# New places for four packed matmul operands, and sixty products that nothing reads

## The chip, the cores and the metric

The kernel runs on one core of one Trainium2 chip. The metric is the device time of one execution in microseconds: the median of the runs of one kernel. One more execution is taken by the hardware profiler; it gives the profile, with times in microseconds from the span's start. TensorE is PE in the profile (PEld is its weight load), VectorE is DVE, ScalarE is ACT, GpSimd is POOL, and SP issues most DMAs.

## What is computed

One layer of a hybrid decoder on 256 tokens, with 16 learned meta tokens in front (272 in all) and 2048 channels, all in float32. The mixer runs two branches on one normalised input: forgetting attention (FoX, 8 heads) and gated linear attention (GLA, 4 heads). Then comes a squared-ReLU MLP of width 8192.

```python
def hybrid_mixer(xn, w_in, b_forget, w_alpha2, b_alpha, gla_norm_g, w_o_fox, w_o_gla, w_out):
    proj = xn @ w_in
    ...
    o_fox = forgetting_attention(fq, fk, fv, ff, b_forget)
    g_log = jax.nn.log_sigmoid((ga @ w_alpha2 + b_alpha).astype(jnp.float32)) / GLA_TAU
    o_gla = gated_linear_attention(gq, gk, gv, g_log)
    o_gla = (head_rmsnorm(o_gla, gla_norm_g) * jax.nn.silu(gr.astype(jnp.float32))).astype(xn.dtype)
    y = jax.nn.sigmoid(gate_fox) * (o_fox @ w_o_fox) + jax.nn.sigmoid(gate_gla) * (o_gla @ w_o_gla)
    return y @ w_out

# reference: h = h + hybrid_mixer(rmsnorm(h), ...);  h = h + squared_relu_mlp(rmsnorm(h), w1, w2)
# squared_relu_mlp: jnp.square(jax.nn.relu(xn @ w1)) @ w2;  at the end rmsnorm(h)[:, N_META:]
```

## The kernel before

**Layout.** Activations stand transposed: channels on the 128 partitions, tokens along the free dimension. A matrix of 2048 rows is 16 row tiles (KT = 16), and the weights come from the host as a stream of 128-column chunks in the order of use; `chunk` counts them. `next_weights` takes the next chunk in two halves of 8 row tiles: SP loads a half (512 KB) into `raw`, ScalarE rounds it to `hi` (L124), and VectorE forms the remainder `lo = raw - hi` (L125), both as float32r. Five `raw` and five `wt` buffers let this run ahead of TensorE.

**Products.** Every activation is split in the same way into a high and a low part that stand side by side, so that one product can stream both. `gemm2` runs 16 steps, and each step (`mac2`) is a pair: `hi` of the weights against high and low activation together, 512 columns (L140), and `lo` against the high activation, 256 columns (L141).

```python
    def mac2(ps, hi, lo, x, first, last):
        nc.tensor.matmul(ps, hi, x, start=first, stop=False)
        nc.tensor.matmul(ps[:, 0:NT], lo, x[:, 0, :], start=False, stop=last)
```

`gemm_all` works on all 272 tokens with three products a step (L157 to L159). The result lies in one accumulator bank of 512 columns, from the pool `pg` (3 banks, the big products) or `px` (5 banks, the small ones). `total` or `add_residual` adds its two halves (ScalarE copies one, VectorE adds).

**The four packed operands.** Besides `x`, the first normalised input, four activations serve as the streamed operand of `gemm2`: `og` (the gated attention's output), `y` (the mixer's sum), `x2` (the second normalised input) and `a` (the squared-ReLU output, made anew for each of four groups of the MLP). Each is 16 pieces of 512 floats, high part and low part without a gap. Two storage slots hold them, one after the other: `s1` holds `x`, then `y`, then `a`; `s2` holds first some scratch, then `og`, then `x2`. In the built program `s1` begins 64 bytes past a multiple of 256 and `s2` 160 bytes past one. `operand` cuts a slot into pieces by a table of places, and `steps` makes that table: piece k starts at `first + 512 * k` floats plus one of four numbers, one for each quarter of the pieces. Before, those four are 0, 64, 128 and 192 floats, all whole multiples of 256 bytes, so that all 16 pieces of a use have one place modulo 256 bytes.

`og` is read by 16 products of 16 pairs (256 pairs), `y` by 16 (256), `x2` by 64 (1024), each of the first three `a` by 16 (256) and the last `a` by 12 (192); its last four output columns go another way, with L850 and L859.

**Order.** The stages run one after the other: the first chunks with the loading of the input, four GLA heads, eight FoX heads, the two output projections with their gates, the product with `w_out`, and four groups of the MLP, each of 16 up and 16 down products. Small work is put off with `later(n, fn)` and issued after n further products; `flush()` issues what is left. `gla_head` ends with `scale`, where `spread` (L223) turns the norm factors (`diag`, VectorE, L220) into a bank from which ScalarE copies `rg` (L586); VectorE then scales `oT` (L589, L591) and both engines split it into `og` (L173, L174). After the fourth head come `flush()`, `og_tile()` and the FoX heads. Within each engine a scheduler of the compiler orders the instructions, so that neighbours in the code can stand apart.

Of the kernel before, what the change touches and what calls it, by code (L numbers as in the profile page):

```python
# [16 lines left out]
P = 128  # L17
# [48 lines left out]
def trunk(ctx: ExitStack, tc: tile.TileContext, hT, w_small, w_all, consts, w_alpha2, out):  # L66
    nc = tc.nc
    serial = [0]

    def nm(s):  # L70
        serial[0] += 1
        return f"{s}_{serial[0]}"
# [7 lines left out]
    px = ctx.enter_context(tc.tile_pool(name="px", bufs=5, space=PSUM))  # L80
# [3 lines left out]
    def bank(pool, s):  # L84
        return pool.tile([P, 512], F32, tag="bank", name=nm(s))
# [7 lines left out]
    def issued():  # L93
        for e in list(waiting):
            e[0] -= 1
            if e[0] <= 0:
                waiting.remove(e)
                e[1]()

    def flush():  # L100
        while waiting:
            issued()
# [26 lines left out]
    def next_weights(keep_hi=None):  # L129
        c = chunk[0]  # L130
        chunk[0] += 1
        parts = []
        for i in range(2):
            hi, lo, step = weight_half(c, i, None if keep_hi is None else keep_hi[:, HK * i : HK * (i + 1), :])
            step(0, HK)
            parts.append((hi, lo))
        return lambda k: (parts[k // HK][0][:, k % HK, :], parts[k // HK][1][:, k % HK, :])
# [5 lines left out]
    def gemm2(w, x, k0=0, nk=KT):  # L143

        ps = bank(pg, "ps")
        for k in range(nk):
            hi, lo = w(k0 + k)
            mac2(ps, hi, lo, x[k], k == 0, k == nk - 1)
        issued()
        return ps  # L150

    def gemm_all(w, x, n=NA):

        ps = bank(pg, "psa")
        for k in range(KT):
            hi, lo = w(k)
            nc.tensor.matmul(ps[:, 0:n], hi, x[:, k, 0, :], start=(k == 0), stop=False)  # L157
            nc.tensor.matmul(ps[:, 0:n], lo, x[:, k, 0, :], start=False, stop=False)  # L158
            nc.tensor.matmul(ps[:, 0:n], hi, x[:, k, 1, :], start=False, stop=(k == KT - 1))  # L159
        issued()  # L160
        return ps

    def total(ps, t=None):

        b = tmp.tile([P, NT], F32, tag="evb", name=nm("evb"))
        nc.scalar.copy(b, ps[:, NT:512])  # L166
        if t is None:
            t = tmp.tile([P, NT], F32, tag="evt", name=nm("evt"), bufs=4)
        nc.vector.tensor_tensor(t, ps[:, 0:NT], b, op=ALU.add)  # L169
        return t  # L170
# [54 lines left out]
    def operand(pool, name, size, places, tag):  # L225


        t = pool.tile([P, size], F32R, tag=tag, name=nm(name))
        rows = []
        for at, gap in places:  # L230
            both = t[:, at : at + 2 * gap].rearrange("p (o t) -> p o t", t=gap) if at + 2 * gap <= size else None
            rows.append(both[:, :, 0:NT])
        return rows

    S1, S2 = 8728, 8628
    def steps(first, *by):
        return [(first + 512 * k + by[k * len(by) // KT], NT) for k in range(KT)]

    AT_OG = steps(8, 0, 64, 128, 192)
    AT_Y = steps(48, 0, 64, 128, 192)  # L240
    AT_X2 = steps(40, 0, 64, 128, 192)
    AT_A = [steps(e, 0, 64, 128, 192) for e in (16, 40, 12, 58)]


    h = keep.tile([P, KT, NA + 3], F32, name="h")
    x = keep.tile([P, KT, 2, NA], F32R, tag="s1", name="x")
# [79 lines left out]
    for s in range(KT // 2):  # L326
# [3 lines left out]
        for kk in range(2):  # L330
            k = 2 * s + kk
# [10 lines left out]
            for c, (hi, lo) in enumerate(at):  # L342
                ps = first_ps[c]
# [5 lines left out]
            for c, (hi, lo) in enumerate(at):  # L349
                ps = first_ps[c]  # L350
# [83 lines left out]
    def og_tile():  # L434
        if not og_box:
            og_box.append(operand(keep, "og", S2, AT_OG, "s2"))
        return og_box[0]

    def gla_gates(ts):
        sg = att.tile([P, 4, NT], F32, tag="sg", name=nm("sg"))  # L440
        for i in range(4):
            t = ts[i] if ts else total(gemm2(next_weights(), xt))
            nc.vector.tensor_tensor(t, t, rbt, op=ALU.mult)
            nc.scalar.activation(sg[:, i, :], t, AF.Sigmoid)
            nc.vector.tensor_tensor(sg[:, i, :], sg[:, i, :], t, op=ALU.mult)
        return sg
# [13 lines left out]
    def gla_head(hd, sg, ready=None):  # L460
# [135 lines left out]
        if sg is None:  # L596
            sg = gla_gates(None)
            st["sg"] = sg
            scale()
        else:  # L600
            st["sg"] = sg
            later(4, scale)
# [8 lines left out]
    ps = gemm_all(lambda k: (small[k // HK][0][:, k % HK, :], small[k // HK][1][:, k % HK, :]), x)  # L611
    norm1_spread()
    nc.vector.tensor_tensor(ga[0:16, :], ps[0:16, 0:NA], rb[0:16, :], op=ALU.mult)
    nc.vector.tensor_tensor(fl, ps[32:40, 0:NA], rb[32:40, :], op=ALU.mult)
    sg0 = gla_gates(ts[0:4])
    table = nc.scalar.preload_act_table_set("natural_log_exp_and_others")
    tc.keep_in_program_order(table)
# [9 lines left out]
    for hd in range(1, GLA_H):  # L627
        gla_head(hd, None)
    flush()
    og = og_tile()  # L630


# [112 lines left out]
    for j0 in range(0, KT, 2):  # L745
        gates = ahead if j0 == 0 else [gate() for _ in range(4)]
        w = next_weights()
        for j in range(2):
            t = total(gemm2(w, oft, k0=8 * j, nk=8))
            nc.vector.tensor_tensor(gates[2 * j], gates[2 * j], t, op=ALU.mult)  # L750
        for j in range(2):
            t = total(gemm2(next_weights(), og))
            nc.vector.tensor_tensor(t, gates[2 * j + 1], t, op=ALU.mult)
            nc.vector.tensor_tensor(yf[:, j0 + j, :], gates[2 * j], t, op=ALU.add)
    y = operand(keep, "y", S1, AT_Y, "s1")
    for j in range(KT):
# [5 lines left out]
    ht = h[:, :, NM:NA]  # L762
    x2 = operand(keep, "x2", S2, AT_X2, "s2")

# [58 lines left out]
    for g in range(NG):  # L823
        a = operand(keep, "a", S1, AT_A[g], "s1")
        held = []
        for f in range(KT):
            ps = gemm2(next_weights(), x2)
# [18 lines left out]
    for n in range(NL):  # L846
        j, ps = KT - NL + n, bank(pg if n < 3 else px, "ps")
# [42 lines left out]
    v, p, none = nc.vector, nc.gpsimd, lambda: None  # L890
# [72 lines left out]
```

## Time and profile before

| | |
|---|---|
| time, median of 2 runs | 1631.84 us (1631.83 to 1631.86) |
| profiled execution | 1631.39 us, span 1629.7 us |
| granted TensorE clock, mean | 0.996 |
| busy: TensorE, weight load | 1612.4 us, 1450.3 us |
| busy: VectorE, ScalarE, GpSimd | 1048.0, 793.7, 91.2 us |
| read from memory | 289.19 MB, 179 GB/s over the span |

Busy time of TensorE is not its pace: matmuls are pipelined, and their ends are modelled. The pace is the time from one start to the next. In the view of windows a row has the stretch, its length, and then for each engine the busy time and the number of instructions (x) that touch the stretch, the granted clock, the busy share of the DMA engines and GB/s.

### The profile page before, as it was taken

Reading aid. Unit: us, or ns where it says so; the run is one execution under the profiler, and the core shown is the slowest. Engines: PE = TensorE matmul, PEld = TensorE weight load, DVE = VectorE, ACT = ScalarE, POOL = GpSimd, SP = SyncE. Lnnn points to the kernel's source line nnn. Section 1 sums busy time; section 2 is a strip of 40 time slices with the busy share of each in tenths; the row PEclk is TensorE's granted clock in tenths of the full one; section 3 lists DMA queues with packets and bytes.
Section 4 is the critical chain, followed back from the end, with each engine's and each line's share of the span. In section 5 each row is a group of like instructions: output and inputs, shape, how many; then the busy total and the mean of one; then the engine's idle time right before and its main releaser. Section 6 shows DMA issues by size and latency. Waiting matters only on the chain.

```text
span 1629.7 us, 25555 instructions
## 1 busy us (share of the span) xinstructions
PE 1612.4 (99%) x9996; PEld 1450.3 (89%) x9996; DVE 1048.0 (64%) x1591; ACT 793.7 (49%) x1217; POOL 91.2 (6%) x144
## 2 busy tenths in 40 slices
PE   8999999999999999999999999999999999999997
PEld 7999999999998888888888888888888888888886
DVE  6766757476556566665677776567656776667655
ACT  6555444454445444444565444444444444444563
POOL 0100000010000000000011000000000000000012
PEclk9999999999999999999999999999999999999998
DMA  8444555454455555555555555555555555555552
GB/s 290 156 143 156 165 161 165 157 195 157 157 161 173 184 191 190 187 191 189 188 189 189 183 190 182 190 186 190 178 197 193 184 188 188 191 184 190 185 193 66
DMA packets 90265, 292.97 MB, mean 180 GB/s; under 512 B 9096, under 2 KB 21648, under 8 KB 89888
## 3 DMA queue, kind: packets, MB, share of 16 engines
q1 hardware_dynamic: 87552, 288.88, 54.1%
q8 instruction: 79, 1.29, 0.3%
q10 hardware_dynamic: 2416, 1.33, 0.3%
q0 software_dynamic: 176, 1.12, 0.2%
q14 instruction: 42, 0.34, 0.1%
HBM read 289.19 MB, written 2.11 MB: 179 GB/s over the span
## 4 chain that ended last, share of the span: by engine, by line
PE 98%; DMA 1%; DVE 0%; ACT 0%; issue 0%; SPq 0%; DVEq 0%; ACTq 0%
PE ps L140 50%; PE ps L141 26%; PE psa L159 5%; PE psa L158 5%; PE psa L157 5%; PE ps L345 1%; PE ps L859 1%; DMA h<-hT_dram 1%; PE pa L506 1%; PE ps L850 0%; PE ps L352 0%; PE po L570 0%; DMA raw<-w_all_dram 0%; PE pz L404 0%; ACT x L332 0%; PE po L571 0%
## 5 line engine op out<-in xcount | busy, mean ns | idle before, releaser
L125 DVE TENSOR_TENSOR wt<-raw,wt 128x1024 fp32r<-128x1024 f32 x522 | 644.7, 1235 | 330.0 <-ACT wt L124 320.0
L124 ACT CAST wt<-raw 128x1024 fp32r<-128x1024 f32 x522 | 548.7, 1052 | 397.3 <-issue 158.6
L140 PE MATMUL ps<-x,wt 128*128 128x512 f32 x1952 | 688.4, 395 | 0.0
L141 PE MATMUL ps<-x,wt 128*128 128x256 f32 x1952 | 551.3, 282 | 0.0
L140 PEld LDWEIGHTS ps<-x,wt 128*128 128x128 f32 x1952 | 366.8, 188 | 83.1
L141 PEld LDWEIGHTS ps<-x,wt 128*128 128x128 f32 x1952 | 367.9, 188 | 0.0
L140 PE MATMUL ps<-a,wt 128*128 128x512 f32 x960 | 336.8, 394 | 0.0
L141 PE MATMUL ps<-a,wt 128*128 128x256 f32 x960 | 270.8, 282 | 0.0
L140 PEld LDWEIGHTS ps<-a,wt 128*128 128x128 f32 x960 | 180.7, 188 | 41.0
L157 PE MATMUL psa<-x,wt 128*128 128x272 f32 x640 | 187.3, 293 | 0.0
L159 PE MATMUL psa<-x,wt 128*128 128x272 f32 x640 | 184.8, 289 | 0.0
L158 PE MATMUL psa<-x,wt 128*128 128x272 f32 x640 | 184.4, 288 | 0.0
L141 PEld LDWEIGHTS ps<-a,wt 128*128 128x128 f32 x960 | 181.5, 189 | 0.0
L166 ACT COPY evb<-ps 128x256 f32<-128x256 f32 x160 | 59.3, 373 | 237.6 <-PE ps L141 235.4
L169 DVE TENSOR_TENSOR evt<-ps,evb 128x256 f32<-128x256 f32 x158 | 66.9, 424 | 107.1 <-ACT evb L166 106.9
L157 PEld LDWEIGHTS psa<-x,wt 128*128 128x128 f32 x640 | 120.3, 188 | 0.7
L158 PEld LDWEIGHTS psa<-x,wt 128*128 128x128 f32 x640 | 120.4, 188 | 0.2
L159 PEld LDWEIGHTS psa<-x,wt 128*128 128x128 f32 x640 | 120.4, 188 | 0.1
L140 PE MATMUL ps<-y,wt 128*128 128x512 f32 x256 | 89.4, 393 | 0.0
L140 PE MATMUL ps<-og,wt 128*128 128x512 f32 x256 | 89.1, 394 | 0.0
L775 ACT COPY evb<-ps 128x256 f32<-128x256 f32 x76 | 28.3, 372 | 113.0 <-PE ps L141 112.9
L141 PE MATMUL ps<-y,wt 128*128 128x256 f32 x256 | 71.7, 280 | 0.0
(261 smaller groups left out, 1396.1 us busy)
## 6 DMA issues: line engine op xcount, KB each, us to landing
raw<-w_all_dram SPq DMA_DIRECT2D x537, 512.0 KB, 3.9
raw<-w_all_dram SPq DMA_DIRECT2D x7, 384.0 KB, 6.8
h<-hT_dram SPq DMA_DIRECT2D x1, 1100.0 KB, 10.0
negc<-fdram POOLq DMA_DIRECT2D x1, 1088.0 KB, 6.0
out_dram<-h SPq DMA_DIRECT2D x3, 256.0 KB, 2.6
out_dram<-h ACTq DMA_DIRECT2D x3, 256.0 KB, 3.1
h<-hT_dram SPq DMA_DIRECT2D x1, 550.0 KB, 7.3
raw<-w_all_dram SPq DMA_DIRECT2D x2, 256.0 KB, 4.4
```

Source lines behind the costliest of these rows:

```text
L124: nc.scalar.copy(hi[:, k, :], r)
L125: nc.vector.tensor_tensor(lo[:, k, :], r, hi[:, k, :].bitcast(F32), op=ALU.subtract)
L140: nc.tensor.matmul(ps, hi, x, start=first, stop=False)
L141: nc.tensor.matmul(ps[:, 0:NT], lo, x[:, 0, :], start=False, stop=last)
L157: nc.tensor.matmul(ps[:, 0:n], hi, x[:, k, 0, :], start=(k == 0), stop=False)
L158: nc.tensor.matmul(ps[:, 0:n], lo, x[:, k, 0, :], start=False, stop=False)
L159: nc.tensor.matmul(ps[:, 0:n], hi, x[:, k, 1, :], start=False, stop=(k == KT - 1))
L166: nc.scalar.copy(b, ps[:, NT:512])
L169: nc.vector.tensor_tensor(t, ps[:, 0:NT], b, op=ALU.add)
L345: nc.tensor.matmul(ps, hi, x[:, k, :, NM:NA], start=st, stop=False)
L506: nc.tensor.matmul(dst, k[:, a, :], q[:, a, :], start=(a == 0), stop=(a == 1))
L775: nc.scalar.copy(b, ps[:, NT:512])
```

## The change

All tables of places change, and a function `pace` is added that runs once, after `flush()`.

```diff
-    AT_OG = steps(8, 0, 64, 128, 192)
-    AT_Y = steps(48, 0, 64, 128, 192)
-    AT_X2 = steps(40, 0, 64, 128, 192)
-    AT_A = [steps(e, 0, 64, 128, 192) for e in (16, 40, 12, 58)]
+    AT_OG = steps(0, 8, 22, 42, 58)
+    AT_Y = steps(0, 6, 22, 36, 52)
+    AT_X2 = steps(0, 10, 26, 44, 60)
+    AT_A = [
+        steps(0, 8, 24, 38, 54),
+        steps(0, 10, 26, 40, 56),
+        steps(0, 12, 28, 42, 60),
+        steps(0, 14, 30, 44, 62),
+    ]
...
+    def pace():
+        flat = x.rearrange("p k o t -> p (k o t)")
+        ps, other = bank(px, "pace"), bank(px, "pace")
+
+        def run(w0, m0, m=P, n=512, step=1, rows=P, banks=(ps,), mv=None):
+            if mv is None:
+                mv = flat[0:rows, m0 : m0 + n * step : step]
+            for i in range(4):
+                nc.tensor.matmul(banks[i % len(banks)][0:m, 0:n], flat[0:rows, w0 : w0 + m], mv, start=True, stop=True)
+
+        run(32, 4128)
+        run(48, 4128)
+        run(48, 4144)
+        run(32, 4144)
+        run(32, 4128, m=32)
+        run(32, 4112, m=32)
+        run(32, 4112)
+        run(32, 4128, n=256)
+        run(32, 4128, n=256, m=32)
+        run(32, 4128, n=128)
+        run(32, 4128, n=128, m=32)
+        run(32, 4128, rows=64)
+        run(32, 4128, step=2)
+        run(32, 4128, banks=(ps, other))
+        run(32, 0, mv=flat[:, 4128:4130].unsqueeze(1).to_broadcast([P, 256, 2]))
...
     flush()
+    pace()
     og = og_tile()
```

With the slots' starts, the places in bytes modulo 256 of the four quarters are:

| operand | before | after |
|---|---|---|
| `og` | 192 | 192, 248, 72, 136 |
| `y` | 0 | 88, 152, 208, 16 |
| `x2` | 64 | 200, 8, 80, 144 |
| `a`, first to fourth group | 128; 224; 112; 40 | 96, 160, 216, 24; 104, 168, 224, 32; 112, 176, 232, 48; 120, 184, 240, 56 |

Each form of `pace` is four products with weights and streamed columns both from `x`, into a bank that nothing reads. The forms differ in the places of the two operands, the number of weight columns (128 or 32), of streamed columns (512, 256, 128), of rows (128 or 64), in the step between columns, in the banks, and in the last one two columns are repeated 256 times by a zero step.

On TensorE, at the end of the last GLA head, the order before goes from the head's last product (`ps`) to the first FoX product (`psa`), and L223 for that head (`pr`) stands 36 products further on, inside it:

```order
L140 MATMUL ps_3453<-x,wt_3449 128x512
L141 MATMUL ps_3453<-x,wt_3449 128x256
L157 MATMUL psa_3545<-x,wt_3536 128x272
L158 MATMUL psa_3545<-x,wt_3536 128x272
L159 MATMUL psa_3545<-x,wt_3536 128x272
...
L223 MATMUL pr_3417<-diag_3493,ones 128x256
```

After the change the same place reads as follows (L452 is the product in `pace`; behind a tile's name stand the weight columns and the streamed columns):

```order
L141 MATMUL ps_3453<-x,wt_3449 128x256
L452 MATMUL pace_3514<-x 128x512 x16
L452 MATMUL pace_3514<-x 32x512 x8
L452 MATMUL pace_3514<-x 128x512 x4
L223 MATMUL pr_3417<-diag_3493,ones 128x256
L452 MATMUL pace_3514<-x 128x256 x4
L452 MATMUL pace_3514<-x 32x256 x4
L452 MATMUL pace_3514<-x 128x128 x4
L452 MATMUL pace_3514<-x 32x128 x4
L452 MATMUL pace_3514<-x 128x512 x9
...
L157 MATMUL psa_3607<-x,wt_3598 128x272
```

The sixty stand between the two products as one block, and L223 has moved out of the first FoX product into the block, behind its 28th. On ScalarE, behind the copy of that last GLA product (`evb`), the row of work before was:

```order
L166 COPY evb_3486<-ps_3453 128x256
L124 CAST wt_3662<-raw_3661 128x8x128
L444 ACTIVATE sg_3234<-evt_3488 128x256
L124 CAST wt_3667<-raw_3666 128x8x128
L586 COPY rg_3233<-pr_3417 128x256
L124 CAST wt_3740<-raw_3739 128x8x128
L173 CAST og_1299<-oT_3231 128x256 x4
```

and it now is (later lines lie 31 lower, so that L475 and L617 are L444 and L586 of before):

```order
L166 COPY evb_3486<-ps_3453 128x256
L124 CAST wt_3724<-raw_3723 128x8x128
L475 ACTIVATE sg_3234<-evt_3488 128x256
L617 COPY rg_3233<-pr_3417 128x256
L173 CAST og_1299<-oT_3231 128x256 x4
L124 CAST wt_3729<-raw_3728 128x8x128
L124 CAST wt_3802<-raw_3801 128x8x128
```

Ahead of the casts into `og` there are now one half of weights (L124) instead of three; the other two stand behind them.

## The prediction, made before the result

> **What bounds the kernel now.** I read the page first: busy shares, granted clock, the chain that ended last.
>
> ```profile
> PE 1612.4 (99%) x9996; PEld 1450.3 (89%) x9996; DVE 1048.0 (64%) x1591; ACT 793.7 (49%) x1217; POOL 91.2 (6%) x144
> PEclk9999999999999999999999999999999999999998
> PE 98%; DMA 1%; DVE 0%; ACT 0%; issue 0%; SPq 0%; DVEq 0%; ACTq 0%
> PE ps L140 50%; PE ps L141 26%; PE psa L159 5%; PE psa L158 5%; PE psa L157 5%; PE ps L345 1%; PE ps L859 1%; DMA h<-hT_dram 1%; PE pa L506 1%; PE ps L850 0%; PE ps L352 0%; PE po L570 0%; DMA raw<-w_all_dram 0%; PE pz L404 0%; ACT x L332 0
> ```
>
> TensorE works 1612 of 1629.7 us at full granted clock, and its own matmuls are 98% of the chain. The second view is TensorE's waits, all of them:
>
> ```profile
> PE pn L223 <- DVE diag L220: 3.5, 1, 3.5
> PE ps L345 <- ACT wt L293: 3.0, 1, 3.0
> PE pn L878 <- ACT sq L866: 1.5, 1, 1.5
> PE warm L318 <- DVE ones L192: 1.3, 1, 1.3
> PE ps L345 <- DVE x L333: 1.0, 1, 1.0
> ```
>
> They come to 10.3 us, and their lines are the start (L318, L345) and the norm at the very end (L878, and the one L223 whose output is `pn`). Between them TensorE waits for nobody. So what is put into the middle of TensorE's program lengthens the kernel one for one, and a matmul form that streams faster or slower moves the end by just as much. The time is the number of products times the pace of each.
>
> A duration in the page is not that pace: the 512-wide product "lasts" 395 ns, but the next starts long before. So I take start to start. The third view is the timeline in one `og` product, its first and its last step of sixteen:
>
> ```profile
> 521.56 0.39 PE L140 MATMUL ps<-og,wt 128*128 128x512 f32 x1
> 521.79 0.27 PE L141 MATMUL ps<-og,wt 128*128 128x256 f32 x1
> 521.91 0.40 PE L140 MATMUL ps<-og,wt 128*128 128x512 f32 x1
> ...
> 526.76 0.40 PE L140 MATMUL ps<-og,wt 128*128 128x512 f32 x1
> ```
>
> One step is a pair, 512 columns against the high weights (L140) and 256 against the low ones (L141). Fifteen pairs lie between 521.56 and 526.76: **346.7 ns a pair**, some 230 ns of it for the 512 (521.56 to 521.79) and 117 for the 256.
>
> **Part 1: the places.** Do places matter at all? The fourth view counts instructions on one operand in stretches where it alone is multiplied: `y` (810:890), `x2` (1260:1340), then the four uses of `a`.
>
> ```profile
> 810.00:890.00 80.00, 80.00 (x460) 70.06 (x459) 0.42 (x1) 0.33 (x1) 1.00 0.57 191
> 1260.00:1340.00 80.00, 80.00 (x458) 70.12 (x457) 0.00 (x0) 0.00 (x0) 1.00 0.57 187
> 990.00:1070.00 80.00, 80.00 (x455) 69.48 (x454) 0.42 (x1) 0.40 (x1) 1.00 0.57 187
> 1170.00:1250.00 80.00, 80.00 (x463) 70.92 (x462) 0.42 (x1) 0.40 (x1) 1.00 0.59 191
> 1350.00:1430.00 80.00, 80.00 (x459) 69.92 (x458) 0.42 (x1) 0.00 (x0) 1.00 0.57 188
> 1526.00:1590.00 64.00, 64.00 (x364) 56.70 (x363) 0.42 (x1) 0.40 (x1) 1.00 0.58 190
> ```
>
> About two of each TensorE count straddle the window's ends; half the rest are pairs. With the place in bytes modulo 256 (slot start plus the table's number):
>
> - `og`, place 192: 346.7 ns; 256 pairs
> - `y`, place 0: 80/229 = 349.3; 256 pairs
> - `x2`, place 64: 80/228 = 350.9; 1024 pairs
> - `a`, place 128: 80/226.5 = 353.2; place 224: 80/230.5 = 347.1; place 112: 80/228.5 = 350.1; 256 pairs each
> - `a`, place 40: 64/181 = 353.6; 192 pairs
>
> The same instruction at the same clock, with nothing waiting, differs by 2% from operand to operand, and the plainest thing that differs is the place. Weighted, these 2496 pairs take 874.3 us, 350.3 ns each.
>
> The change scatters them over 28 places, all multiples of 8; 192, 224 and 112 are among them, the other 25 are new. What a new place costs no row shows. From both sides by the nearest rows: all at the best pace seen (346.7) gives 865.4 us, **9 us less**; all at the worst (353.6) gives 882.6, **8 us more**. I see no order in the seven numbers that I would trust (112 and 128 are neighbours and differ by 3 ns), so I take for each new place their plain mean, 350.1, the middle of the two ends. Then `og` loses 0.9 us (256 x 3.4 ns), the second `a` 0.8, `y` 0.2; `x2` gains 0.8 (1024 x 0.8 ns), the uses at 128 and 40 gain 0.8 and 0.7, and `a` at 112 stays: the sum is **-0.4 us, between -9 and +8**. Behind them 192 single products of the tail (L850, L859) read the last `a` too; 3 ns each way would be 0.6 us, and I leave it in the range. Twenty-five independent draws also average out: the seven paces scatter by 2.7 ns, `x2` has its 1024 pairs in four draws of 256 and the rest have 64 or 48 in each, which makes 1.6 us of scatter in the sum.
>
> One rule speaks against any effect. The Trainium skill, "TensorE: Matmul & The Clock Gate", section "Step-by-step: what each phase is for", gives TensorE two independent read ports, so that loading the next weights takes nothing from the running matmul; an operand's place would then be indifferent. The rows above do not bear that out: 346.7 against 353.6 ns. By the rule the term is 0 instead of -0.4, so the sum would be 0.4 us higher.
>
> The writers of these tiles (L173, L174, L795, L796) also write to other places. In the trace ScalarE and VectorE are at 49% and 64%, no L140 or L141 stands among TensorE's waits, and these writes do not set the end; I cost them at nothing. If the cover went, it would show as a wait on these lines.
>
> **Part 2: the sixty products.** Each form is four products. They read `x`, complete since the first stage, and write two accumulator banks that are free. By the order they stand where TensorE went straight from L141 to L157, so there is no gap for them to fill:
>
> ```profile
> 333.04 0.39 PE L140 MATMUL ps<-x,wt 128*128 128x512 f32 x1
> 333.27 0.28 PE L141 MATMUL ps<-x,wt 128*128 128x256 f32 x1
> 333.39 0.29 PE L157 MATMUL psa<-x,wt 128*128 128x272 f32 x1
> ```
>
> All of their time counts. Eleven forms are 512 wide (44 products), two 256 (8), two 128 (8).
>
> - 512 wide: the rows above give 230 or 231 ns (333.04 to 333.27): 44 x 0.231 = **10.2 us**.
> - 256 wide: 333.27 to 333.39 is 120 ns and in `og` 117; 8 x 0.119 = **1.0 us**.
> - 128 wide: only the plain fp32 transposes are as narrow:
>
> ```profile
> 358.12 0.27 PE L696 MATMUL pv<-cons,vT 128*128 128x128 f32 x1
> 358.23 0.27 PE L697 MATMUL pv<-cons,vT 128*128 128x128 f32 x1
> 358.34 0.27 PE L698 MATMUL pv<-cons,vT 128*16 128x128 f32 x1
> ```
>
> 110 ns each. I take 110 for the four with 128 weight columns and 70, between that row and half a 256, for the four with 32: **0.7 us**.
>
> Sum **11.9 us**. What no row shows: 32 weight columns, 64 rows, a stride of two, a pair of columns repeated by a zero step, two banks in turn. Low end: extra columns alone cost (231 - 119)/256 = 0.44 ns each; if the rest vanished, 512 would take 224, 256 take 112 and 128 take 56, together 11.2 us. High end: the strided and the repeated form stream at half pace, 8 x 0.23 = 1.9 us more, and the narrow ones take a 256's time, 0.2 us more: 14.0. I take 11.9, nearest to the rows that most of the products match. On the stride a page has a rule: the Trainium skill, "SBUF — State Buffer", section "Door 1: The DMA port swizzle", puts full bandwidth at two or more hits in a 16-byte line, and every second fp32 column gives just two. No run here shows it; by it the strided form costs nothing extra and the high end falls by 0.9 us.
>
> What is queued behind them? L223, the norm factors of the last gated head, now stands behind the 28th product instead of in the first FoX product. It needs VectorE's `diag`:
>
> ```profile
> 334.85 0.48 DVE L220 TENSOR_SCALAR diag<-cons,ry 128x128 f32<-128x128 f32 x2
> 337.90 0.59 PE L223 MATMUL pr<-diag,ones 128*128 128x256 f32 x2
> ```
>
> 28 products at 0.23 us after 333.39 are 339.8; `diag` is ready at 335.3, so TensorE does not wait. Then `rg` (L586) and the casts into `og` come about 2 us later than now, and `og` is first read at 521 us. On ScalarE two weight halves, of the third and the fourth FoX product, move behind the casts into `og`; the first two products have theirs before the sixty end. SP's transfers keep their order. Everything after simply starts 11.9 us later.
>
> **Sum.** Profiled time 1631.39 us (span 1629.7 and 1.7 around it), 0.45 below the median 1631.84. 1631.39 + 11.9 - 0.4 = 1642.9 for a profiled execution, and against the median **1643.3 us**, 0.7% slower. That is under the 2% (33 us) that I treat as about what a measurement of this kernel can tell from no change.
>
> **Rivals.**
>
> - *The new places win the products back* (not slower than before). The 2496 pairs would have to give 11.9 us, 4.8 ns each, so 345.5 ns on average, below the best place in the trace. Against it: 192 and 224 read 346.7 and 347.1, as if at a floor. All places at that floor give 1634.7. Only a place faster than any seen gets below 1631.8. Chance 0.03 for under 1634.7.
> - *A start off a 16-byte line breaks the stream* (slower than 2%). Of the 28 places 15 are 8 past a multiple of 16, with 1296 of the pairs. To pass 33 us with the 11.9, each of those pairs must cost 16 ns more, 366 ns; at 373 ns the time is 1673. Against it: place 40 is such a place and reads 353.6, equal to 128 within 0.4 ns. It is one place, though, and the costliest. A mild form, all fifteen at 353.6 and the rest near 349, adds 3 us to the 1643.7 without the mean's gain. Chance 0.03 for the strong form, 0.15 for the mild (1647).
> - *Strided and repeated columns at half pace*: 1645.2. No row for or against. Chance 0.15.
> - *The change does not do what it says* (the sixty are dropped): the rows of the order show them in the built program. Then 1631.8; chance 0.01.
>
> **How the numbers follow.** The forecast, with the products within 1 us of 11.9 and the places within 3 us of zero, has 0.63. Predicted 1643.3. Its own range is 1640 to 1647; to the mild and the half-pace cases the range reaches up to 1649, and for places that turn out better than the mean down to 1638: outside are the strong cases, 0.06, and the ends of the others. Faster by over 2%: 0.01; slower by over 2%: 0.03; within: 0.96.
>
> **What would show it.** In the timeline after 333 us sixty `pace` products at 0.22 to 0.24 us each in the 512 forms, one block of 11 to 14 us, L223 in it without an idle time before it. In the windows on `a`, `x2` and `y` a count between 453 and 463 in 80 us; inside one product of sixteen steps the pair changes at every fourth step. TensorE's list of waits stays as it is. Wrong would be: a wait on an L140, a pair outside 346 to 354 ns, or a `pace` form far from its row.

## The result, and the profile after

The changed kernel takes **1651.15 us** (median of two runs, 1650.90 and 1651.40), 1.0118 times the time before with a 95% interval of 1.0075 to 1.0162, so it is slower by less than 2%. The forecast was 1643.3, its range 1638 to 1649: slower was right, the size was 8 us short. The profiled execution takes 1650.9 us, its span is 19.5 us longer than before.

Page of the changed kernel: busy shares, granted clock, chain that ended last.

```profile
span 1649.2 us, 25676 instructions
PE 1634.0 (99%) x10056; PEld 1464.1 (89%) x10056; DVE 1048.0 (64%) x1591; ACT 793.8 (48%) x1217; POOL 88.7 (5%) x144
PEclk9999999999999999999999999999999999999998
PE 98%; DMA 1%; DVE 1%; ACT 0%; issue 0%; SPq 0%; DVEq 0%; ACTq 0%
```

Sixty matmuls more (10056 against 9996), the same clock, TensorE still 98% of the chain. Its list of waits, whole:

```profile
PE pn L223 <- DVE diag L220: 3.5, 1, 3.5
PE pn L910 <- ACT sq L898: 1.5, 1, 1.5
PE warm L323 <- DVE ones L192: 1.3, 1, 1.3
PE ps L350 <- ACT wt L298: 1.1, 1, 1.1
PE ps L350 <- DVE x L338: 0.6, 1, 0.6
PE ps L357 <- DVE wt L299: 0.2, 1, 0.2
```

No L140, L141 or L452 stands in it. The lines at the start (L350, L357; L345 before) wait 1.9 us together instead of 4.0. So the 19.5 us are pace, not waiting. Where do they lie? First the block of sixty, in the timeline (start in us, length, engine, line, how many):

```profile
332.71 6.64 PE L452 MATMUL pace<-x 128*128 128x512 f32 x28
339.19 0.59 PE L223 MATMUL pr<-diag,ones 128*128 128x256 f32 x2
339.43 6.82 PE L452 MATMUL pace<-x 128*128 128x256 f32 x32
346.09 0.29 PE L157 MATMUL psa<-x,wt 128*128 128x272 f32 x1
```

From 332.71 to 346.09 are 13.4 us (the name of the third row is that of its first form). L223 was in the program before too, where it cost the same 0.4 us, so the sixty take **12.95 us**. The block begins 0.7 us earlier than the FoX product began before (333.39).

Then the four operands. The windows of the changed kernel, on `y`, on `x2` (named `x` there), on the four uses of `a`:

```profile
824.00:904.00 80.00, 80.00 (x455) 69.87 (x455) 0.42 (x1) 0.16 (x1) 1.00 0.58 189
1275.00:1355.00 80.00, 80.00 (x454) 69.93 (x453) 0.00 (x0) 0.00 (x0) 1.00 0.57 187
1005.00:1085.00 80.00, 80.00 (x455) 69.86 (x454) 0.42 (x1) 0.40 (x1) 1.00 0.57 186
1188.00:1268.00 80.00, 80.00 (x454) 69.76 (x453) 0.26 (x1) 0.00 (x0) 1.00 0.57 186
1368.00:1448.00 80.00, 80.00 (x459) 70.03 (x458) 0.42 (x1) 0.16 (x1) 1.00 0.59 190
1546.00:1610.00 64.00, 64.00 (x366) 55.98 (x365) 0.42 (x1) 0.41 (x1) 1.00 0.58 190
```

TensorE's counts: `y` fell from 460 to 455, `x2` from 458 to 454, the second `a` from 463 to 454. One instruction of a count is 0.8 ns a pair, too coarse for a sum, so the table has the mean of the times from one L140 to the next in the two traces (without two of `x2`, over 420 ns in both, where other work stands between):

| use | pairs | before, ns | after, ns | difference, us |
|---|---|---|---|---|
| `og` | 256 | 346.7 | 352.2 | +1.4 |
| `y` | 256 | 348.9 | 352.9 | +1.0 |
| `x2` | 1024 | 351.1 | 354.0 | +3.0 |
| `a`, first to fourth | 256, 256, 256, 192 | 353.3; 346.7; 350.0; 353.4 | 353.1; 353.8; 350.2; 351.8 | 0.0; +1.8; +0.1; -0.3 |

The places cost **+7.0 us**, where the prediction had -0.4. 12.95 + 7.0 - 0.7 = 19.3 of the 19.5.

Inside a product the pace changes at every fourth step. One product of the first `a` (places 96, 160, 216, 24), the first step of each quarter and of the product behind it:

```profile
1046.66 0.39 PE L140 MATMUL ps<-a,wt 128*128 128x512 f32 x1
...
1048.05 0.39 PE L140 MATMUL ps<-a,wt 128*128 128x512 f32 x1
...
1049.45 0.40 PE L140 MATMUL ps<-a,wt 128*128 128x512 f32 x1
...
1050.89 0.40 PE L140 MATMUL ps<-a,wt 128*128 128x512 f32 x1
...
1052.32 0.39 PE L140 MATMUL ps<-a,wt 128*128 128x512 f32 x1
```

Four pairs each: 1.39, 1.40, 1.44, 1.43 us, that is 347.5, 350, 360 and 357.5 ns a pair. From the third of the sixteen products on, each repeats this within 1 ns a pair. The first two do not: the second reads 347.5, 352, 354.5 and 350.8 at the same four places.

### The profile page after: what moved, and what is told of

The parts are those of the page before. It is cut to its first block, busy times and chain, and to the rows that moved or that the text cites. A ratio compares the mean times of both kernels' runs of the same rounds, so it can differ in the third digit from the quotient of the medians.

```text
span 1649.2 us, 25676 instructions
## 1 busy us (share of the span) xinstructions
PE 1634.0 (99%) x10056; PEld 1464.1 (89%) x10056; DVE 1048.0 (64%) x1591; ACT 793.8 (48%) x1217; POOL 88.7 (5%) x144
## 3 DMA queue, kind: packets, MB, share of 16 engines
q0 software_dynamic: 176, 1.12, 0.2%
## 4 chain that ended last, share of the span: by engine, by line
PE 98%; DMA 1%; DVE 1%; ACT 0%; issue 0%; SPq 0%; DVEq 0%; ACTq 0%
PE ps L140 50%; PE ps L141 26%; PE psa L159 5%; PE psa L158 5%; PE psa L157 5%; PE ps L891 1%; PE ps L350 1%; PE pace L452 1%; DMA h<-hT_dram 1%; PE pa L537 1%; PE ps L357 0%; PE ps L882 0%; PE po L601 0%; DMA raw<-w_all_dram 0%; PE pz L409 0%; PE po L602 0%
## 5 line engine op out<-in xcount | busy, mean ns | idle before, releaser
L124 ACT CAST wt<-raw 128x1024 fp32r<-128x1024 f32 x522 | 548.6, 1051 | 406.7 <-issue 160.2
L140 PE MATMUL ps<-x,wt 128*128 128x512 f32 x1952 | 691.5, 397 | 0.0
L141 PE MATMUL ps<-x,wt 128*128 128x256 f32 x1952 | 550.9, 282 | 0.0
L140 PEld LDWEIGHTS ps<-x,wt 128*128 128x128 f32 x1952 | 368.7, 189 | 84.4
L141 PEld LDWEIGHTS ps<-x,wt 128*128 128x128 f32 x1952 | 369.9, 189 | 0.0
L140 PE MATMUL ps<-a,wt 128*128 128x512 f32 x960 | 338.4, 395 | 0.0
L141 PE MATMUL ps<-a,wt 128*128 128x256 f32 x960 | 270.1, 281 | 0.0
L140 PEld LDWEIGHTS ps<-a,wt 128*128 128x128 f32 x960 | 181.1, 189 | 42.7
L141 PEld LDWEIGHTS ps<-a,wt 128*128 128x128 f32 x960 | 181.2, 189 | 0.0
L140 PE MATMUL ps<-og,wt 128*128 128x512 f32 x256 | 90.5, 395 | 0.0
L140 PE MATMUL ps<-y,wt 128*128 128x512 f32 x256 | 90.4, 395 | 0.0
L141 PE MATMUL ps<-og,wt 128*128 128x256 f32 x256 | 72.1, 282 | 0.0
```

The costliest lines, as they stand in the source:

```text
L124: nc.scalar.copy(hi[:, k, :], r)
```

## The experiments

**Do the two parts add?** One run without the call of `pace`, one with the old tables and the sixty.

```diff
     flush()
-    pace()
     og = og_tile()
```

> The changed kernel without the sixty products; the 28 places stay. The traces so far put the block of products at 13.4 us of which about 0.45 is L223, and the seven uses at +7.1 us. If the two parts add up, this kernel takes 1651.15 - 12.9 = 1638.2 us, 6.4 above the kernel before. If the products also disturb what follows (the order of the next products, the weights' lead), it takes less, down to 1631.8; if they cover something, more.

> The kernel before with the sixty products, its old places kept. If the parts add up: 1631.84 + 12.9 = 1644.7 us, and the uses of og, y, x2 and a keep 346.6, 348.9, 351.1, 353.3, 346.7, 350.0 and 353.4 ns a pair. By my prediction's term for the products, 1643.7.

Places alone: **1638.76 us**, 1.0043 [1.0031, 1.0056], 7.0 us above the 1631.72 of the kernel before in these runs. Products alone: **1644.45 us**, 1.0077 [1.0065, 1.0090], 12.7 us above it. 7.0 + 12.7 = 19.7, against 19.3 for both by the medians (1651.15 - 1631.84): they add, and neither disturbs the other.

**Does the place set the pace?** The kernel before with other tables: in one run all seven uses at place 192, in the other each use at one place 8 past a multiple of 16.

```diff
-    AT_Y = steps(48, 0, 64, 128, 192)
-    AT_X2 = steps(40, 0, 64, 128, 192)
-    AT_A = [steps(e, 0, 64, 128, 192) for e in (16, 40, 12, 58)]
+    AT_Y = steps(32, 0, 64, 128, 192)
+    AT_X2 = steps(8, 0, 64, 128, 192)
+    AT_A = [steps(e, 0, 64, 128, 192) for e in (32, 32, 32, 32)]
```

> The kernel before, no products, all seven uses at place 192 in all four quarters. If the place sets the pace (own pace, or company: both keep a uniform use as it was), every use comes to 346.6 ns as og had: 2496 pairs x (350.3 - 346.6) = 9 us less, 1622.6 us. If the pace belongs to the tile, its slot or its neighbours in time and not to the place, y, x2 and a keep 349, 351 and 350 to 353, and the time stays at 1631.8.

> The kernel before, no products, each use uniform at one place that read badly among its four in the changed kernel: og 72, y 152, x2 8, a 216, 24, 104, 136; all are 8 past a multiple of 16. Own pace: each keeps what its quarter read (358.1, 356.9, 355.7, 359.2, 356.5, 353.6, 352.1), 2496 pairs at 356.1 on average, 14.5 us more than before: 1646. Company (a place is slow only because its neighbours have another): each falls back to between 346.6 and 353.4, the time to 1632 give or take 4. Line (a start off a 16-byte line costs, and always the same): all seven read alike, near the mean of the fifteen such quarters, 354, which gives 1641.

All at 192: **1621.82 us**, 0.9940 [0.9926, 0.9953], faster than both kernels. Its windows on `y` and the first two `a`:

```profile
808.00:888.00 80.00, 80.00 (x463) 69.95 (x463) 0.42 (x1) 0.40 (x1) 1.00 0.57 189
985.00:1065.00 80.00, 80.00 (x463) 69.94 (x462) 0.42 (x1) 0.40 (x1) 1.00 0.58 191
1163.00:1243.00 80.00, 80.00 (x463) 69.98 (x462) 0.42 (x1) 0.40 (x1) 1.00 0.58 191
```

463 everywhere; by the starts every use runs at 346.7 ns. Off the line: **1645.44 us**, 1.0084 [1.0070, 1.0098]; windows on `y` (152) and on `a` (216, 24, 104):

```profile
812.00:892.00 80.00, 80.00 (x450) 69.93 (x449) 0.42 (x1) 0.40 (x1) 1.00 0.56 186
994.00:1074.00 80.00, 80.00 (x447) 69.12 (x446) 0.42 (x1) 0.40 (x1) 1.00 0.56 182
1180.00:1260.00 80.00, 80.00 (x450) 69.96 (x449) 0.42 (x1) 0.40 (x1) 1.00 0.56 185
1360.00:1440.00 80.00, 80.00 (x463) 70.84 (x463) 0.42 (x1) 0.40 (x1) 1.00 0.58 190
```

Same instructions, same clock, 23.6 us between the two runs: the place matters. But 8 past a line is no rule: 216 runs at 359.9 ns, 24 and 152 at 356.7, 8 at 355.7, and 104, just as far off it, at the floor of 346.7. The 1646 us written for the case that each quarter's pace is its place's own came close partly by luck: 104 fell from the 353.6 of its quarter to 346.7, while 72 rose from 358.1 to 360.0.

**A price list?** The kernel before with 32 products of sixteen pairs added ahead of the FoX heads, read from `x` at every multiple of 8, weights at 192; nothing reads them, here and in the four probes below, each of which was executed once.

```diff
+        for m in range(0, 256, 8):
+            for k in range(16):
+                pair(k, 16, m, 192)
```

> The kernel before, with 32 extra products of 16 pairs behind the gated attention that nothing reads, one at each place modulo 256 that is a multiple of 8; weights and streamed columns both from x, weights at place 192. Own pace: the places already seen in uniform use read again what they read there (192, 224, 104: 346.7 ns; 0: 349; 112: 350; 64: 351; 40, 128, 136: 353.3; 8: 355.7; 24, 152: 356.7; 72, 216: 360), and the rest fill the gaps with the mean near 352. Line: the 16 places that are 8 past a multiple of 16 stand apart from the other 16. If the pace belongs to the stage and not to the place, all 32 read alike.

The 32 paces run from 346.6 to 360.0 ns (pairs 3 to 16). The sixteen places on a 16-byte line average 350.0 ns, the sixteen off it 353.5, so there is a tendency; but 192, 208, 224, 232, 240 and 248 are all at 346.6 to 346.9, and 56 and 72 at 360. Against the uses in whole kernels it fails three times: place 0 has 353.6 here and 348.9 in `y` before, 24 has 350.0 here and 356.7 above, 104 has 355.6 here and 346.7 above. One place, two paces. A list cannot be right.

**The company.** Products with several places, each product three times:

```diff
+        for q in ((192, 224, 192, 224), (192, 104, 192, 104), (104, 168, 224, 32), (32, 224, 168, 104),
+                  (96, 160, 216, 24), (24, 96, 24, 96), (192, 248, 72, 136), (192, 192, 192, 192)):
+            for _ in range(3):
```

> The kernel before, with 8 sets of three extra products of 16 pairs that nothing reads, the place changing every four pairs. Own pace alone: a quarter keeps its uniform pace, so 192/224 and 192/104 in turn stay at 346.7 and the order of 104, 168, 224, 32 does not matter. Company: a change of place costs a few ns over the next pairs whatever the two places are; 192/104 in turn then reads 348 to 352, and the reversed order gives the quarters other values than the order of the changed kernel did (104: 353.6, 224: 350.8 there, 346.7 uniform).

In the last of the three products, 192 and 224 in turn take 348.4 ns, though each alone had 346.6. 192 and 104 in turn take 352.5. 104, 168, 224, 32 take 354.1, the same four in reverse 350.9. All at 192: 346.7. But 24 and 96 in turn take 351.7, just the mean of 356.7 and 346.7, paces that the two also have alone, so a change of place does not always cost something. What stands ahead matters, and by how much depends on the places. This is carried into the kernel by two runs: the changed places with each use's four in reverse order (without `pace`), and the kernel before with all uses at four places that are equally fast alone, 192, 208, 224, 240.

```diff
-    AT_X2 = steps(0, 10, 26, 44, 60)
+    AT_X2 = steps(0, 60, 108, 154, 202)
```

> The changed kernel without the sixty products, and with the four places of every use in reverse order: og 136, 72, 248, 192, x2 144, 80, 8, 200, and so on. The places and their shares are those of the run with the places alone (1638.8 us). If a place has its price whatever stands before it, the time is the same, 1638.8 within 1 us, and every quarter keeps its pace. If the pace of a quarter also hangs on what was streamed ahead of it, it is not: in the probe the product 104, 168, 224, 32 took 354.1 ns a pair and its reverse 350.9, and 3.2 ns on all 2496 pairs are 8 us, so the time may be anywhere from 1631 to 1647, with the paces of the quarters exchanged or new.

> The kernel before with all seven uses at four places of equal pace, 192, 208, 224 and 240, one for each quarter (each alone took 346.6 ns a pair in the probe of 32 places). If only the place counts, this is as fast as all at 192: 1621.8 us. If a change of place within a product costs something by itself, it is slower: by the alternating product of the probe (192 and 224, 348.4 ns a pair) 2496 x 1.7 ns = 4.2 us more, 1626.0.

Reversed: **1634.35 us**, 1.0019 [1.0009, 1.0028], 4.4 us less than in the order of the change with the very same places (4.2, each counted from the kernel before in the same set of runs); `x2` goes from 354.0 to 350.1 ns, its quarter at 144 alone from 356.1 to 350.3. Four floor places: **1627.93 us**, 0.9979 [0.9969, 0.9988], 6.1 us more than all at 192 (4.2 were expected). One product of its first `a`, first steps of the quarters:

```profile
1059.34 0.39 PE L140 MATMUL ps<-a,wt 128*128 128x512 f32 x1
...
1060.73 0.40 PE L140 MATMUL ps<-a,wt 128*128 128x512 f32 x1
...
1062.13 0.39 PE L140 MATMUL ps<-a,wt 128*128 128x512 f32 x1
...
1063.53 0.39 PE L140 MATMUL ps<-a,wt 128*128 128x512 f32 x1
...
1064.93 0.39 PE L140 MATMUL ps<-a,wt 128*128 128x512 f32 x1
```

347.5, 350, 350, 350 ns: between these four places the changes cost 2.4 ns a pair on average, and 2496 pairs at 349.1 instead of 346.7 (means by the starts) are 6.0 us. It is no price for every change: the quarter at 80 in the reversed `x2` runs at 345.4 ns, below any settled pace.

**Why two paces at one place?** Each of four places six times, entered in six ways: behind the product before it, or behind one single matmul of 64 to 320 columns.

```diff
+        for m in (104, 24, 0, 192):
+            for ahead in (0, 64, 128, 192, 256, 320):
+                if ahead:
+                    one(0, 192, n=ahead)
+                for k in range(16):
+                    pair(k, 16, m, 192)
```

> The kernel before with 24 products of sixteen pairs from x that nothing reads, weights at 192: streamed places 104, 24, 0 and 192, each place six times, ahead of them nothing or one single product of 64, 128, 192, 256 or 320 columns. If the place fixes the pace, the six agree to 0.5 ns: 355.6 or 346.7 at 104, 350 or 356.7 at 24, 353.6 at 0, 346.7 at 192. If a place has several steady rhythms and the entry picks one, the six differ at 104 and at 24 (the two values each that the probe and the kernel have shown), and 192 stays at 346.7.

Timeline, fourth and last step of a product, twelve pairs apart: 104 entered plainly, 104 behind the 64 columns; 192 plainly, 192 behind 128 columns.

```profile
333.94 0.39 PE L446 MATMUL pace<-x 128*128 128x512 f32 x1
...
338.19 0.40 PE L446 MATMUL pace<-x 128*128 128x512 f32 x1
...
340.13 0.39 PE L446 MATMUL pace<-x 128*128 128x512 f32 x1
...
344.29 0.39 PE L446 MATMUL pace<-x 128*128 128x512 f32 x1
...
437.66 0.39 PE L446 MATMUL pace<-x 128*128 128x512 f32 x1
...
441.82 0.39 PE L446 MATMUL pace<-x 128*128 128x512 f32 x1
...
448.99 0.40 PE L446 MATMUL pace<-x 128*128 128x512 f32 x1
...
453.23 0.40 PE L446 MATMUL pace<-x 128*128 128x512 f32 x1
```

4.25 against 4.16 us, and 4.16 against 4.24: by the unrounded starts 355.0 and 346.7 ns at 104, 346.7 and 353.3 at 192. Over all entries 104 runs at 355 five times and at 346.7 once; 24 at 350 three times and at 356.7 three times; 0 at 348.9 three times and at 353.3 three times; 192 at 346.7 four times and at 353.3 twice. The first steps differ, then the product locks into a repeating rhythm (at 104: 364, 354, 351, 351 ns) and stays in it. So **a place has more than one steady rhythm, and the entry picks one.** The expectation that 192 stays at 346.7 missed.

**Weights.** The streamed places 192, 128, 72, 0, 104 against weights at six places:

```diff
+        for w in (0, 64, 104, 128, 200, 224):
+            for m in (192, 128, 72, 0, 104):
+                for k in range(16):
+                    pair(k, 16, m, w)
```

> The kernel before, with 30 extra products of 16 pairs that nothing reads: streamed columns at 192, 128, 72, 0, 104 against weights at 0, 64, 104, 128, 200, 224. Two ports that do not meet: the weights' place changes nothing, and each column place keeps 346.7, 353.3, 360, 349, 346.7 in all six. Collision of the two reads: the pace follows the difference of the two places, so 128 against 128 and 0 against 0 come to 346.7 as 192 against 192 did, and 72 against 200 reads as 64 against 192 did, 351.

Every streamed place changes with the weights: 72 from 353.3 to 360.0, 104 from 347.0 to 359.5, 192 from 346.7 to 353.7. It looks like an effect of the weights' place, but each product was also entered in another way, and the entry alone does as much; this probe cannot part the two. The forecast of the collision, that equal places read 346.7, holds for 128 against 128 (346.7) and fails for 0 against 0 (353.3).

**Which read loses the time?** Single forms, sixteen each, at four streamed places: 512 and 256 columns, 128 and 32 weight columns, and two columns repeated.

```diff
+        for m in (192, 72, 128, 24):
+            for n, cols, same in ((512, P, False), (512, 32, False), (256, P, False), (256, 32, False), (512, P, True)):
+                for k in range(16):
+                    one(k, m, 192, n, cols, same)
```

> The kernel before, with extra products that nothing reads, 16 in a row of one form, at places 192, 72, 128 and 24: 512 or 256 columns against 128 or 32 weight columns, and two columns repeated 256 times. If the lost time is a collision with the load of the weights, 32 weight columns lose most of it (512 in 218 ns at every place). If it is the columns' own read, 32 weight columns keep the difference between the places and only the repeated columns lose it, 215 to 220 ns, as the changed kernel's last form read.

Timeline: two of the repeated form at 192, thirteen apart, then two of the plain form at 72, twelve apart.

```profile
346.57 0.38 PE L452 MATMUL pace<-x 128*128 128x512 f32 x1
...
349.38 0.38 PE L452 MATMUL pace<-x 128*128 128x512 f32 x1
...
350.04 0.40 PE L452 MATMUL pace<-x 128*128 128x512 f32 x1
...
352.84 0.40 PE L452 MATMUL pace<-x 128*128 128x512 f32 x1
```

Repeated: 2.81/13 = 216 ns, the same at all four places. Plain: 2.80/12 = 233 ns; 228 at 192, 233 to 234 at 128 and 24. With 32 weight columns it stays at 229 to 232, but the order of the places is not kept: 192 is now at 232 and 72 at 229. So loading a quarter of the weights gives back at most 4 ns, and at 192 it costs 4; streaming two columns over and over gives 12 to 18 ns. That points to the reading of fresh columns as the place where the time is lost. It is not fully shown: the repeated form also differs in its access pattern, and no run parts the two.

## Why the prediction was wrong

**The products: right mechanism, one term short.** The sixty stand as one block of 13.4 us with L223 in it (11 to 14 was named), they delay the end one for one, and nothing that moved behind them became a wait. They take 12.95 us instead of 11.9. The missing part is the strided form. In the changed kernel's timeline, 22 contiguous products apart (eight of them with 32 weight columns), then two strided ones apart, then two repeated ones apart:

```profile
333.63 0.39 PE L452 MATMUL pace<-x 128*128 128x512 f32 x1
...
338.72 0.39 PE L452 MATMUL pace<-x 128*128 128x512 f32 x1
...
342.92 0.63 PE L452 MATMUL pace<-x 128*128 128x512 f32 x1
...
343.82 0.64 PE L452 MATMUL pace<-x 128*128 128x512 f32 x1
...
345.22 0.38 PE L452 MATMUL pace<-x 128*128 128x512 f32 x1
...
345.66 0.38 PE L452 MATMUL pace<-x 128*128 128x512 f32 x1
```

Contiguous 231 ns, as costed; strided **450 ns**, half pace; repeated 220. Four strided products at 0.22 us more are 0.9 us, nearly the whole difference; by the starts the four on 64 rows add another 0.2 (1.12 us instead of 0.92). The rival of half pace (chance 0.15) was right for the stride and wrong for the repetition. The Trainium skill, "SBUF — State Buffer", section "Door 1: The DMA port swizzle", has full bandwidth at two or more hits in a 16-byte line; at 450 against 231 ns the trace does not agree for TensorE's reads.

**The places: the step that failed** is "I take for each new place their plain mean, 350.1", and with it that 25 draws average out to 1.6 us. It took the pace for a property of the place and the seven uses for a sample of it. Those seven each stream one place through all their products and have settled in one rhythm; the new tables change the place every four steps. The runs show three things in its stead: a place has several rhythms (104: 346.7 or 355); a change of place can cost something even between places that are equally fast alone (2.4 ns a pair at 192, 208, 224 and 240); and the order of the same four places moves the kernel by over 4 us. `x2`, with 1024 pairs, has the largest share: +3.0 us, where the step gave -0.8. How the 7.0 us divide between worse places and the changes is not settled: it would need a price for each place, and there is none. An estimate from the 32 settled paces of the probe gives 875.4 us for the old places, where 874.2 were measured, and 877.8 for the new ones in any order; measured are 881.2 in the order of the change and 876.9 in reverse.

**The bounds held and the range did not use them.** -9 to +8 us stood in the text; the measured +7.0 lies inside. That is partly luck: the bounds were the ends of seven settled uses, and the run off the line costs 13.7 us by places alone. It is luck too that 1631.4 + 11.9 + 8 gives 1651, the measured time, since the parts are 12.95 and 7.0. The range stopped at 1649 because the draws were taken as independent and centred.

**The rivals.** The mild form of "off a 16-byte line" came nearest with 1647: weighted by pairs the fifteen off-line places average 354.1 ns in the changed kernel (353.6 was written), but the others average 351.4 (without the steps of 388 ns below) and not 349, and place 104 at the floor shows that the line is not the cause. "Back to the floor" did not come with these tables; 1634.7 without the sixty's 11.9 would be 1622.8, and the run with all uses at 192 gave 1621.8.

**What would show it.** The counts, the change at every fourth step and the absence of a wait on L140 came as written. Two signs of being wrong came true. One is a pair outside 346 to 354: quarters at 360 and 357.5 in the product shown. The other is a `pace` form far from its row: the strided one. In the second `a` one step, the third at place 32, even takes 388 ns in fifteen of the sixteen products, with no wait in the list. The Trainium skill, "TensorE: Matmul & The Clock Gate", section "Step-by-step: what each phase is for", says of its two independent read ports that loading the next weights takes nothing from the running matmul. With 32 weight columns in place of 128 a 512-wide product stays at 229 to 232 ns, against 228 to 234, so the trace does not speak against that. That the place of the streamed operand would then be indifferent was the prediction's own step, and 1621.8 against 1645.4 us for places alone says it is not.

## What to carry to other kernels

Where TensorE is the chain, the place of the streamed operand modulo 256 bytes is a knob worth some per cent of the pace (346.7 to 360 ns a pair), but it is tuned in the whole kernel and not from a list: give all pieces of an operand one place, try a few, and read the pace from start to start. A mean over uses that have each settled is no forecast for a use that changes every few steps; where the bounds of a term are wide and its mechanism is unknown, let the range reach them. Keep the streamed columns contiguous: every second column halved the pace here.

## What the runs showed of the hardware beyond that

- The steady paces of a pair repeat from place to place: 346.7, 350, 353.3, 356.7 and 360 ns are the commonest, and nothing steady was seen below 346.5. Within a rhythm single pairs go from 340 to 366 ns, in cycles of one to seven pairs.
- 512 columns take 216 ns if two columns are repeated, 228 to 233 contiguous, 450 with a step of two.
- What makes a rhythm is open. That the entry picks it and that it then lasts to the end of the product was measured. That the time is lost in reading fresh columns is argued from two forms, and which part of the chip keeps the rhythm was not measured.
